# Strassen's algorithm in the up product of a squared-ReLU MLP

## The chip, the cores and the metric

The kernel runs on one core of a Trainium2 chip. The metric is the device time of one execution in microseconds (us); three executions of the kernel before took 1535.1, 1535.53 and 1536.06 us, and the median, 1535.53 us, is the time before. The profile is one more execution, taken by the hardware profiler; its own clock runs from the first to the last instruction (the span).

TensorE (PE) multiplies a stationary tile of 128x128 with a moving tile of 128 rows and up to 512 columns and adds into one of eight PSUM banks. VectorE (DVE), ScalarE (ACT) and GpSimd (POOL) do everything else; GpSimd works on SBUF only here. SyncE (SP) issues the loads.

## The reference

A trunk of two layers over 512 positions with 1024 channels, all in float32. Layer 0 mixes with a gated DeltaNet, layer 1 with a Conformer convolution; each layer then attends to a memory of 256 positions and ends in the MLP, which is what changes here:

```python
def sq_relu_mlp(h, w_up, w_down):      # w_up 1024 x 4096, w_down 4096 x 1024
    return jnp.square(jax.nn.relu(h @ w_up)) @ w_down

h = h + sq_relu_mlp(rms_norm(h, mlp_norm[layer]), mlp_w_up[layer], mlp_w_down[layer])
```

## The kernel before, in words

Activations lie transposed: a tile holds 128 channels (partitions) by 512 positions, so `h` is eight tiles. Every product is made of three fp32r matmuls (`mm3`, L227): each float32 operand is split into a high part, rounded to fp32r, and a low part, the rest. ACT writes the high part and DVE the low one: `split` (L264) for activations, `wsplit` (L199) for weights. So a product of one weight tile of 128x128 with one activation tile costs three matmuls of 512 columns, at the lines L229, L230 and L231.

**Weights.** All weight halves of the program stand in one list, `order`, in the order of their use. `wload` (L191) loads one of 512 KB (128x1024, eight stationary tiles, or 24 matmuls) into one of `NRAW`=3 buffers `raw`; `wsplit` turns it into `wh` and `wl`, of which there are `NW`=3 each. `wnext` (L217) hands out the next unit, and asks for loads `NRAW`+2 units and for splits `NW` units ahead. A buffer is given again when its last matmul is done, so a weight split in the trace is released by a matmul.

**MLP** (`mlp`, L960). The 4096 hidden channels are four groups of 1024. `MLP_ORDER` (L1426) runs up 0, up 1, down 0, up 2, down 1, up 3, down 2, down 3. An up step makes eight hidden tiles: 24 matmuls into one bank (`proj`, L237, over eight k-tiles), then `up_ev` (L966): DVE reads the bank, takes the positive part and multiplies it with the row `rb` of RMS factors; ACT squares; `split` makes `uh` and `ul`. A down step makes eight output tiles, 24 matmuls each, and DVE adds the bank to the residual. The RMS factor commutes with the product, so the up product starts on unnormalised activations: `Norm.parts` (L312) makes `xh`, `xl` (gain applied) as each residual tile appears at the end of the attention, and `stat` and `spread` compute `rb` while the first up tiles are multiplied.

**The last group** (`finish`, L1364). In layer 1 the last down step is done with positions on the partitions: eight outputs of 128 positions by 512 channels, each of four transposes (residual) and 24 matmuls, then the final norm and the store. Its weights are loaded and split by `load` (L1358) into the pool of general slots (`NSLOT`=69 tiles of 128x512).

The code is written in program order; a scheduler orders the instructions of each engine by that order and by its own estimate of when operands and buffers are ready, and sets all waits. The engines run their queues in order.

Of the kernel before, what the change touches and what calls it, by code (L numbers as in the profile page):

```python
# [14 lines left out]
P = 128  # L15
# [23 lines left out]
def tile_trunk(ctx, tc, xT, memT, prm_d, adt_d, bdw_d, tap_d, fin_d, w_ab, w_kq, w_v, w_z, w_dno, w_pw1, w_pw2,  # L39
# [159 lines left out]
    def wsplit():  # L199
        u = ws["split"]  # L200
        ws["split"] += 1
        while ws["load"] <= u:
            wload()
        raw = ws["raw"].pop(u)
        h = wp.tile([P, 1024], F32R, tag="wh", name=nm("wh"), bufs=NW)
        lo = wp.tile([P, 1024], F32R, tag="wl", name=nm("wl"), bufs=NW)
        ins = [act.copy(h, raw)]  # L207
# [7 lines left out]
        ws["hl"][u] = (h, lo)  # L215

    def wnext(key, hf):  # L217
# [9 lines left out]
    def mm3(ps, wk, xk, first, last):  # L227
        (wh, wl), (xh, xl) = wk, xk
        pe.matmul(ps, wh, xh, start=first, stop=False)  # L229
        pe.matmul(ps, wh, xl, start=False, stop=False)  # L230
        pe.matmul(ps, wl, xh, start=False, stop=last)  # L231
# [119 lines left out]


# [606 lines left out]

    def mlp(layer, norm, hres, nxt, mid=None, end=None, pre=None):  # L960
        xs = norm.xs
        hid = {}
        cur = list(hres)
        st = {"first": []}

        def up_ev(g, i, ps):  # L966
            t = slot(s="rl")
            stt(t, ps, 0.0, norm.rb, ALU.max, ALU.mult)
            u = slot(s="u2")
            act.activation(u, t, AF.Square)  # L970
            hid.setdefault(g, []).append(split(u, "u"))

        for kind, g in MLP_ORDER:
            if (kind, g) == ("dn", 3) and mid is not None:
                mid()
            if (kind, g) == ("dn", 3) and end is not None:
                return end(hid[3], cur)
            for i in range(8):
                w = wnext((kind, layer, g * 4 + i // 2), i % 2)
                ps = psum(kind)  # L980
                if kind == "up":
                    proj(w, xs, ps)
                    if g == 0 and i < 2:
                        st["first"].append(ps)
                        if i == 0:
                            norm.stat()
                        else:
                            norm.spread()
                            for j in range(2):
                                up_ev(0, j, st["first"][j])  # L990
                    else:
                        up_ev(g, i, ps)
                else:
                    proj(w, hid[g], ps)
                    if pre is not None and (g, i) in PRE:
                        pre()
                    hn = slot(s="h")
                    if g == 3:
                        tt(dve, by_phase(hn), phased(ps), phased(cur[i]), ALU.add)
                        nxt.add(i, hn)  # L1000
                    else:
                        tt(dve, hn, ps, cur[i], ALU.add)
                    cur[i] = hn
# [341 lines left out]
    n2 = Norm("mlp_norm0")  # L1345
# [5 lines left out]
    n5 = Norm("mlp_norm1")  # L1351
# [12 lines left out]
    def finish(hid, cur):  # L1364
        gt = fsp.tile([P, 1024], F32, tag="fs", name=nm("gt"))
        nc.sync.dma_start(out=gt, in_=fin_d.partition_broadcast(P))
        st = {}
        for c, g in LAST:
            if len(ws_) < 16:
                load()  # L1370
            cs, gs = slice(c * P, (c + 1) * P), slice(g * 512, g * 512 + 512)
            ps = psum("dn")
            for j in range(4):
                pe.matmul(ps[:, j * P:(j + 1) * P], cur[4 * g + j][:, cs], ident, is_transpose=True, start=j == 0, stop=False)
            for k in range(KT):
                (xh, xl), (h, lo) = hid[k], ws_[8 * g + k]
                pe.matmul(ps, xh[:, cs], h, start=False, stop=False)
                pe.matmul(ps, xl[:, cs], h, start=False, stop=False)
                pe.matmul(ps, xh[:, cs], lo, start=False, stop=k == KT - 1)
# [3 lines left out]
            if g == 0:  # L1383
# [4 lines left out]
                continue  # L1388
# [8 lines left out]

    mlp(1, n5, h, None, None, finish, load)


NSLOT = 69
NCV = 6
NRAW = 3
PRE = ((2, 4), (2, 6))
# [6 lines left out]
NW = 3  # L1411
# [14 lines left out]
MLP_ORDER = [("up", 0), ("up", 1), ("dn", 0), ("up", 2), ("dn", 1), ("up", 3), ("dn", 2), ("dn", 3)]  # L1426
# [12 lines left out]
def _pack_a(np, w, order=None):  # L1439
    t = _tiles_a(np, w)  # L1440
    if order is not None:
# [31 lines left out]
def _layout(np, i):  # L1473
# [34 lines left out]
    r["w_up"] = np.stack([_pack_a(np, i["mlp_w_up"][j]) for j in range(2)])  # L1508
# [20 lines left out]
```

## Time and profile before

| | |
|---|---|
| median of three executions | 1535.53 us |
| span of the profiled execution | 1533.4 us |
| PE busy | 1511.9 us, 99% |
| DVE, ACT, POOL busy | 900.1, 676.3, 228.7 us |
| mean granted PE clock | 0.996 |
| share of the 16 DMA engines | 29.6% |

The profile gives no time for the profiled execution beside its span; the median lies 2.1 us above that span, which is what comes before the first and after the last instruction.

A matmul's row shows its modelled duration; matmuls overlap, so what one of them costs is the distance between the starts of two that follow each other. The MLP of layer 0 runs from 492 us to 846 us, that of layer 1 from 1174 us to the end. In a row of the groups stand line, engine, operation, output and inputs, shape and count, then the sum in us and the mean in ns, then the idle time before and who ended it.

### The profile page before, as it was taken

The page shows a single profiled execution, that of the slowest core. Times are in us where ns is not written, and L with a number is a line of the kernel's source. Part 1 is how long each engine was busy: PE and PEld are TensorE (multiplying, and loading weights), DVE is VectorE, ACT ScalarE, POOL GpSimd, SP SyncE. Part 2 cuts the span into 40 slices and gives each one's busy share as a digit, 9 for nine tenths or more (in the row PEclk, how much of TensorE's full clock was granted, in tenths as well). Part 3 has the DMA queues.
Part 4 walks back from the last instruction along what each step waited for, and adds up shares of the span by engine and source line. Part 5 has one row for each costly group of instructions (what it writes and reads, how often), then busy time and mean ns, then how long its engine had stood idle before and what let it go on. Part 6 is the DMA issues. An engine that isn't in the chain of part 4 may idle for free.

```text
span 1533.4 us, 19367 instructions
## 1 busy us (share of the span) xinstructions
PE 1511.9 (99%) x7560; PEld 1274.0 (83%) x7560; DVE 900.1 (59%) x1372; ACT 676.3 (44%) x1089; POOL 228.7 (15%) x231
## 2 busy tenths in 40 slices
PE   9999999999999999999999999899999999999998
PEld 7888888988888888888888889878888888888886
DVE  6898898766545543443445599864554543434441
ACT  6847655655434442332324464363443441323332
POOL 1421220103112000000003685302112000000000
PEclk9999999999999999999999999999999999999999
DMA  5321123342213222222234524422212222232231
GB/s 179 100 82 62 60 76 111 124 152 82 74 37 110 96 97 97 96 96 97 96 109 150 180 85 149 155 95 96 74 51 97 97 96 97 96 98 97 99 106 55
DMA packets 49051, 153.56 MB, mean 100 GB/s; under 512 B 6208, under 2 KB 8000, under 8 KB 48960
## 3 DMA queue, kind: packets, MB, share of 16 engines
q1 hardware_dynamic: 48960, 152.33, 29.6%
q8 instruction: 59, 0.97, 0.2%
q14 instruction: 32, 0.26, 0.1%
HBM read 149.42 MB, written 2.10 MB: 99 GB/s over the span
## 4 chain that ended last, share of the span: by engine, by line
PE 78%; ACT 1%; DVE 1%; DMA 0%; POOL 0%; issue 0%; ACTq 0%; POOLq 0%; DVEq 0%
PE up L229 8%; PE up L231 8%; PE up L230 8%; PE dn L230 7%; PE dn L231 7%; PE dn L229 7%; PE pw L229 3%; PE pw L231 3%; PE pw L230 3%; PE q L229 2%; PE xo L230 2%; PE q L231 2%; PE q L230 2%; PE xo L229 2%; PE xo L231 2%; PE cv L1130 1%
## 5 line engine op out<-in xcount | busy, mean ns | idle before, releaser
L207 ACT CAST wh<-raw 128x1024 fp32r<-128x1024 f32 x248 | 260.0, 1051 | 627.3 <-PE dn L230 190.4
L70 DVE TENSOR_TENSOR wl<-raw,wh 128x1024 fp32r<-128x1024 f32 x224 | 275.9, 1233 | 96.3 <-ACT wh L207 94.7
L229 PE MATMUL up<-xh,wh 128*128 128x512 f32 x512 | 199.4, 389 | 0.0
L231 PE MATMUL up<-xh,wl 128*128 128x512 f32 x512 | 199.2, 389 | 0.0
L230 PE MATMUL up<-xl,wh 128*128 128x512 f32 x512 | 199.2, 389 | 0.0
L231 PE MATMUL dn<-uh,wl 128*128 128x512 f32 x448 | 174.3, 389 | 0.0
L229 PE MATMUL dn<-uh,wh 128*128 128x512 f32 x448 | 174.3, 389 | 0.0
L230 PE MATMUL dn<-ul,wh 128*128 128x512 f32 x448 | 174.3, 389 | 0.0
L70 DVE TENSOR_TENSOR h<-dn,h 128x512 f32<-128x512 f32 x56 | 41.8, 747 | 163.3 <-PE dn L231 163.3
L73 DVE SCALAR_TENSOR_TENSOR rl<-up,rb 128x512 f32<-128x512 f32 x64 | 44.2, 691 | 153.6 <-PE up L231 153.6
L70 POOL TENSOR_TENSOR sq<-sq,sq 128x512 f32<-128x512 f32 x30 | 48.6, 1621 | 470.1 <-ACT sq L321 470.1
L230 PEld LDWEIGHTS up<-xl,wh 128*128 128x128 f32 x512 | 96.1, 188 | 20.0
L231 PEld LDWEIGHTS up<-xh,wl 128*128 128x128 f32 x512 | 96.1, 188 | 20.0
L229 PEld LDWEIGHTS up<-xh,wh 128*128 128x128 f32 x512 | 96.1, 188 | 20.0
L229 PEld LDWEIGHTS dn<-uh,wh 128*128 128x128 f32 x448 | 84.1, 188 | 17.5
L230 PEld LDWEIGHTS dn<-ul,wh 128*128 128x128 f32 x448 | 84.1, 188 | 17.4
L231 PEld LDWEIGHTS dn<-uh,wl 128*128 128x128 f32 x448 | 84.1, 188 | 17.4
L73 DVE SCALAR_TENSOR_TENSOR ca<-x,prm,ca 128x512 f32<-128x512 f32 x120 | 87.9, 751 | 2.9 <-ACT ca L1093 1.3
L229 PE MATMUL h<-xh,wh 128*128 128x512 f32 x192 | 77.5, 404 | 1.2 <-ACT xh L314 1.2
L230 PE MATMUL h<-xl,wh 128*128 128x512 f32 x192 | 75.5, 393 | 0.6 <-DVE xl L73 0.6
L231 PE MATMUL h<-xh,wl 128*128 128x512 f32 x192 | 75.4, 393 | 0.0
L70 POOL TENSOR_TENSOR wl<-raw,wh 128x1024 fp32r<-128x1024 f32 x24 | 59.1, 2466 | 50.0 <-ACT wh L207 38.2
(348 smaller groups left out, 3068.0 us busy)
## 6 DMA issues: line engine op xcount, KB each, us to landing
raw<-w_up SPq DMA_DIRECT2D x64, 512.0 KB, 3.4
raw<-w_dn SPq DMA_DIRECT2D x64, 512.0 KB, 3.5
raw<-w_pw SPq DMA_DIRECT2D x24, 512.0 KB, 3.6
raw<-w_kq SPq DMA_DIRECT2D x16, 512.0 KB, 3.7
raw<-w_k SPq DMA_DIRECT2D x16, 512.0 KB, 3.8
raw<-w_vv SPq DMA_DIRECT2D x16, 512.0 KB, 3.8
raw<-w_q SPq DMA_DIRECT2D x16, 512.0 KB, 3.5
raw<-w_o SPq DMA_DIRECT2D x16, 512.0 KB, 3.5
```

Of the source, the lines that this page charges most:

```text
L70: return e.tensor_tensor(out=o, in0=a, in1=b, op=op)
L73: dve.scalar_tensor_tensor(out=o, in0=a, scalar=s, in1=b, op0=op0, op1=op1)
L207: ins = [act.copy(h, raw)]
L229: pe.matmul(ps, wh, xh, start=first, stop=False)
L230: pe.matmul(ps, wh, xl, start=False, stop=False)
L231: pe.matmul(ps, wl, xh, start=False, stop=last)
L1130: pe.matmul(o, x, TAPS[m][2 * j + u // 4][:, (u % 4) * P:(u % 4 + 1) * P], start=u == 0, stop=False)
```

## The change

The up product of a pair of hidden tiles (256 channels) is a product of 2x2 blocks: the weights A11, A12 (first hidden tile; even and odd k-tiles) and A21, A22 (second hidden tile), each four stationary tiles, and the activations B11, B12, B21, B22 (even or odd k-tile; positions 0-255 or 256-511), each 256 columns wide. The Winograd form of Strassen's algorithm makes it with seven block products instead of eight:

- `FormNorm.parts` replaces `Norm.parts` for the two MLPs. After each second residual tile it makes the activation forms B11, B21, B22, P1 = B11-B12, T3 = B22-B12, P2 and T4 (further sums), each as a high and a low part.
- `wforms` replaces `wsplit` for up weights. Per pair, POOL makes four sums of 128x512 (S2, S1, S3, S4), and `wpair` splits three blocks of 128x1024 and one of 128x512.
- `Up.run` does one block product: 4 k-tiles x 3 matmuls of 256 columns. Seven products go into three banks per pair: A takes the products 1, 6, 7 and 4 on top of each other, and is read after each of them; B takes 2; C takes 5 and then 3, and is read after 7 and after 3.
- The two hidden tiles of the pair are then made by `scalar_tensor_tensor` with `rb`, squared and split as before (the sign of the second is turned, and `min` taken for `max`).
- The order is written out: the seven products of four pairs a, b, c, d, interlaced, the first six k-tiles of three down tiles at the end of each group (`d006`), and the last down tile of the group before at its start (`d704p`). The groups run up 0, down 0, up 1, down 1 and so on. `finish` is cut into steps so that its first outputs fit into that order.
- Buffers: `NRAW` 3 to 4, `NW` 3 to 4 (splits are still asked for 3 units ahead, loads 6), `NSLOT` 69 to 70; the DMA scratch is set to 1024. The k-tiles of `w_up` are stored even ones first.

The core of the diff:

```diff
+    def wpair(src, names):
+        h = wp.tile([P, 1024], F32R, tag="wh", name=nm("wh"), bufs=NW)
+        lo = wp.tile([P, 1024], F32R, tag="wl", name=nm("wl"), bufs=NW)
+        act.copy(h, src)
+        tt(dve, lo, src, h.bitcast(F32), ALU.subtract)
+        return {n: (h[:, i * 512:i * 512 + 512], lo[:, i * 512:i * 512 + 512]) for i, n in enumerate(names)}
+
+    def wforms(raw, hf):
+        if hf == 0:
+            ws["first"] = raw
+            return wpair(raw, ("A11", "A12"))
+        top = ws.pop("first")
+        a11, a12, a21, a22 = top[:, 0:512], top[:, 512:1024], raw[:, 0:512], raw[:, 512:1024]
+        sa = fsp.tile([P, 1024], F32, tag="fs", name=nm("sa"))
+        sb = fsp.tile([P, 1024], F32, tag="fs", name=nm("sb"))
+        tt(pool, sa[:, 512:1024], a21, a22, ALU.add)
+        tt(pool, sa[:, 0:512], sa[:, 512:1024], a11, ALU.add)
+        r = wpair(sa, ("S2", "S1"))
+        tt(pool, sb[:, 0:512], a11, a21, ALU.add)
+        tt(pool, sb[:, 512:1024], sa[:, 0:512], a12, ALU.add)
+        r.update(wpair(sb, ("S3", "S4")))
...
+        r["A22"] = h, lo
+        return r
-        while ws["load"] < min(i + NRAW + 2, len(order)):
+        while ws["load"] < min(i + 6, len(order)):
-        while ws["split"] < min(i + (NW if i else 1), len(order)):
+        while ws["split"] < min(i + (3 if i else 1), len(order)):
...
+    class FormNorm(Norm):
+        def parts(self, t, h):
+            xg = slot(s="xg")
+            act.activation(xg, h, AF.Copy, scale=pc(self.g, t))
+            if t % 2 == 0:
+                self.even = xg
+                return
+            e, o = self.even, xg
+            b = slot(F32R, "xb")
+            act.copy(b[:, 0:256], e[:, 0:256])
+            tt(dve, b[:, 256:512], e[:, 0:256], b[:, 0:256].bitcast(F32), ALU.subtract)
+            g1, g2 = slot(s="g1"), slot(s="g2")
+            tt(dve, g1[:, 0:256], e[:, 0:256], e[:, 256:512], ALU.subtract)
+            tt(dve, g1[:, 256:512], o[:, 256:512], e[:, 256:512], ALU.subtract)
+            stt(g2[:, 0:256], g1[:, 0:256], -1.0, o[:, 256:512], ALU.mult, ALU.subtract)
+            stt(g2[:, 256:512], g2[:, 0:256], -1.0, o[:, 0:256], ALU.mult, ALU.subtract)
+            f = {"B11": (b[:, 0:256], b[:, 256:512])}
+            for src, n0, n1 in ((o, "B21", "B22"), (g1, "P1", "T3"), (g2, "P2", "T4")):
+                h_, l_ = split(src, "xf")
...
+    PAIR = {1: ("A", "A11", "B11", True), 2: ("B", "A12", "B21", True), 3: ("C", "S4", "B22", False),
+            4: ("A", "A22", "T4", False), 5: ("C", "S1", "P1", True), 6: ("A", "S2", "P2", False),
+            7: ("A", "S3", "T3", False)}
...
+        def run(self, n, p):
...
+            ps = s[bank][:, 0:256]
+            wh, wl = s["w"][wf]
+            for k in range(4):
+                c = slice(k * P, (k + 1) * P)
+                mm3(ps, (wh[:, c], wl[:, c]), self.norm.xs[k][xf], first and k == 0, k == 3, not first)
...
+            if n == 1:
+                act.copy(mu[:, lo], ps)
+            elif n == 2:
+                tt(dve, c1[:, lo], ps, mu[:, lo], ALU.add)
+            elif n == 6:
+                act.copy(mu[:, hi], ps)
+            elif n == 7:
+                act.copy(r[:, hi], ps)
+                tt(dve, r[:, hi], s["C"][:, 0:256], r[:, hi], ALU.add)
+            elif n == 4:
+                stt(r[:, lo], ps, 0.0, rb[:, lo], ALU.min, ALU.mult)
+                stt(r[:, hi], r[:, hi], 0.0, rb[:, hi], ALU.min, ALU.mult)
+                self.out(2 * p + 1, r)
+            elif n == 3:
+                tt(dve, c1[:, hi], ps, mu[:, hi], ALU.add)
+                stt(c1, c1, 0.0, rb, ALU.max, ALU.mult)
+                self.out(2 * p, c1)
...
-NSLOT = 69
+NSLOT = 70
-NRAW = 3
+NRAW = 4
-NW = 3
+NW = 4
-MLP_ORDER = [("up", 0), ("up", 1), ("dn", 0), ("up", 2), ("dn", 1), ("up", 3), ("dn", 2), ("dn", 3)]
+UP_TAIL = "7c 1d 2d 4c 6d 5d 3c 7d d006 4d d106 3d d206"
+UP_FIRST = "1a 5a 1b 5b 2a 6a stat 2b 6b spread 1c 7a 2c 7b 4a 6c 4b 5c 3a " + UP_TAIL.replace("7c ", "7c 3b ", 1)
+UP_SEQ = "d704p 1a 2a 6a d748p 5a 7a 1b 2b 4a 6b 5b 3a 7b 1c 2c 4b 6c 5c 3b " + UP_TAIL
+UP_LAST = UP_SEQ.replace("7c", "pre 7c").replace("5d", "pre 5d")
+MLP_ORDER = [(kind, g) for g in range(4) for kind in ("up", "dn")]
```

More of the change, by code (lines that the diff above doesn't have):

```diff
@@ L204, in wsplit @@
         raw = ws["raw"].pop(u)
+        if order[u][0][0] == "up":
+            ws["hl"][u] = wforms(raw, order[u][1])
+            return
         h = wp.tile([P, 1024], F32R, tag="wh", name=nm("wh"), bufs=NW)
@@ L1396, in finish, with step @@
             nc.sync.dma_start(out=yT[cs, 512:1024], in_=y)
+        def step(n, head):
+            if n is not None:
+                if n < 2:
+                    load()
+                mms(n, 0, 6)
+                return
+            gt = fsp.tile([P, 1024], F32, tag="fs", name=nm("gt"))
+            nc.sync.dma_start(out=gt, in_=fin_d.partition_broadcast(P))
+            st["gt"] = gt
+            for n in range(8):
+                mms(n, 6 if n < 3 else 0, KT)
+                out(n)
+        return step
     mlp(1, n5, h, None, None, finish, load)
-NSLOT = 69
+NSLOT = 70
 NCV = 6
-NRAW = 3
-PRE = ((2, 4), (2, 6))
+NRAW = 4
 DN_ORDER = (("k", 0), ("q", 0), ("z", 0), ("v", 0), ("k", 1), ("q", 1), ("z", 1), ("v", 1))
```

166 lines of the change are left out of this document (105 added, 61 removed).

## The prediction

> **What bounds the kernel now.** I read the page's head first, then the busy time by stretches, then the waits of PE, the groups by shape, and the timeline at a few places.
>
> ```profile
> span 1533.4 us, 19367 instructions
> PE 1511.9 (99%) x7560; PEld 1274.0 (83%) x7560; DVE 900.1 (59%) x1372; ACT 676.3 (44%) x1089; POOL 228.7 (15%) x231
> ```
> ```profile
> 541.00:628.00 87.00, 87.00 (x385) 72.06 (x384) 35.89 (x40) 26.09 (x32) 0.00 (x0) 1.00 0.29 97
> ```
> ```profile
> PE cvT L1114 <- ACT ca L1099: 4.7, 1, 4.7
> ```
>
> The second row is a stretch of up 1 and down 0 of layer 0 (columns PE, PEld, DVE, ACT, POOL, then clock, DMA share, GB/s). PE is busy throughout, at full clock; 384 matmuls in 87.00 us are 226.6 ns each. In the whole program PE is idle for 21.5 us (1533.4 - 1511.9), and its longest wait, 4.7 us, is in the Conformer. No wait of PE lies inside an MLP. So time here is the number of matmuls times their spacing, and DVE (35.89 of 87) and ACT (26.09) have room.
>
> **The price of a narrow matmul.** The change makes fewer multiplications but more matmuls: the question is what 256 columns cost. The trace has that shape, with weights stationary, in the memory's key projection.
>
> ```profile
> L229 PE MATMUL up<-xh,wh 128*128 128x512 f32 x512 | 199.4, 389 | 0.0
> L229 PE MATMUL K<-mh,wh 128*128 128x256 f32 x128 | 37.0, 289 | 0.0
> ```
> ```profile
> 950.05 0.28 PE L230 MATMUL K<-ml,wh 128*128 128x256 f32 x1
> ...
> 955.57 0.28 PE L231 MATMUL K<-mh,wl 128*128 128x256 f32 x1
> ```
>
> 47 matmuls start from the first to the last of these rows: 5.52 us / 46 = 120.0 ns. That is 6.7 ns over half of 226.6.
>
> Before: 3 x 512 = 1536 up matmuls x 226.6 ns = 348.1 us. After: 2 layers x 16 pairs x 7 products x 4 k-tiles x 3 = 2688 x 120.0 ns = 322.6 us. **PE: -25.5 us.** An eighth of the work would be 43.5 us; 18 go to the fixed part of each matmul (at 129.5 ns nothing would be left).
>
> [...]
>
> **What the other engines get.** The rows by which I price it:
>
> ```profile
> L207 ACT CAST wh<-raw 128x1024 fp32r<-128x1024 f32 x248 | 260.0, 1051 | 627.3 <-PE dn L230 190.4 <-PE up L230 184.2 <-issue 124.2
> L70 DVE TENSOR_TENSOR wl<-raw,wh 128x1024 fp32r<-128x1024 f32 x224 | 275.9, 1233 | 96.3 <-ACT wh L207 94.7
> L70 DVE TENSOR_TENSOR ul<-u,uh 128x512 fp32r<-128x512 f32 x64 | 44.3, 692 | 5.8 <-ACT uh L266 5.5
> L970 ACT ACTIVATE u<-rl 128x512 f32<-128x512 f32 x64 | 40.1, 626 | 9.6 <-DVE rl L73 9.6
> L266 ACT CAST uh<-u 128x512 fp32r<-128x512 f32 x64 | 39.8, 622 | 2.1
> L801 ACT COPY mrs<-mrs 128x256 f32<-128x256 f32 x1 | 0.4, 373 | 2.7 <-PE mrs L300 2.7
> L70 DVE TENSOR_TENSOR dg<-ident,vl 128x256 fp32r<-128x256 f32 x1 | 0.4, 422 | 0.0
> L70 POOL TENSOR_TENSOR sq<-sq,sq 128x512 f32<-128x512 f32 x30 | 48.6, 1621 | 470.1 <-ACT sq L321 470.1
> L70 DVE TENSOR_TENSOR h<-dn,h 128x512 f32<-128x512 f32 x56 | 41.8, 747 | 163.3 <-PE dn L231 163.3
> ```
>
> Per pair of hidden tiles, in us:
> - DVE: low parts of weights 3 x 1.23 + 0.69; five reads or products of 256 columns, 5 x 0.42; one of 512, 0.69; two `ul`, 1.38. Together 8.6 (before 2 x (1.23 + 0.69 + 0.69) = 5.2).
> - ACT: 3 x 1.05 + 0.62; three bank copies, 1.1; two squares and casts, 2.5. Together 7.4 (before 4.6).
> - POOL: four sums, 4 x 1.62 = 6.5 (before nothing).
>
> PE's own time for a pair is 7 x 12 x 0.12 = 10.1 us, so none of them is over it alone. But two share a road:
>
> ```profile
> 465.13 1.35 POOL L70 TENSOR_TENSOR sq<-sq,sq 128x512 f32<-128x512 f32 x1 [17.20 <-ACT sq L321]
> ...
> 831.83 2.39 POOL L70 TENSOR_TENSOR wl<-raw,wh 128x1024 fp32r<-128x1024 f32 x1 [2.37 <-ACT wh L207]
> 832.76 2.02 DVE L73 SCALAR_TENSOR_TENSOR xl<-h,prm,xh 128x512 fp32r<-128x512 f32 x1 [0.79 <-ACT xh L314]
> 834.17 1.75 POOL L70 TENSOR_TENSOR sq<-sq,sq 128x512 f32<-128x512 f32 x1
> ```
> ```profile
> L73 DVE SCALAR_TENSOR_TENSOR xl<-x,prm,xh 128x512 fp32r<-128x512 f32 x8 | 5.4, 748 | 0.0
> L73 DVE SCALAR_TENSOR_TENSOR ca<-x,prm,ca 128x512 f32<-128x512 f32 x120 | 87.9, 751 | 2.9 <-ACT ca L1093 1.3
> ```
>
> `xl`, two SBUF operands, takes 0.75 us alone and 2.02 beside a POOL sum: it ends half a us after POOL does. The POOL sum behind it takes 1.75 for 1.35. They run one after the other. `ca`, whose sum lies in PSUM, keeps 751 ns in the Conformer, where POOL is busy too. So POOL's time must be added to DVE's wherever DVE works on SBUF.
>
> Stretch by stretch: from `d704p` to `d206` a group takes PE 5.4 (down 7) + 40.3 (28 products) + 12.2 (54 matmuls) = 58.0 us. DVE has there 4 x 8.6, four down weights (4.9) and one residual (0.7): 40. POOL has 4 x 6.5 = 26 with contention, or 4 x 4 x 1.35 = 21.6 without. Were all of POOL's time lost to DVE, 62 to 66 us would stand against 58. But DVE is idle or reading PSUM for 18 + 7 of the 58 us, so some 0.57 of POOL's time (33/58), 15 us, should hit it: 55, no backlog. The sums of pair a can besides be made under the four down tiles before. A form is moreover split about 7 us ahead of its use: with four `wh` tiles, the block A of pair c finds the buffer of block A of b when `2b` ends, five products (7.2 us) before `1c`, and needs 1.05 + 1.23 us. **Steady stretch: 0, at most 8 us per group** (66 - 58).
>
> Bank A is read by ACT between its products. The tightest place is `1a 2a 6a`: one product, 1.44 us, for a copy of 0.37 that can sit behind a cast of 1.05. At most 0.2 us per group.
>
> What was covered and is no longer: before, up g+1 (43 us) lay between up g and down g. Now `u` of the last pair must be ready for the k-tiles 6 and 7 of `d0`. From the end of `3d`: bank read 0.42, product 0.69, square 0.63, cast 0.62, low part 0.69, with five hand-overs of about 0.15: 3.8 us. `d206` covers 4.1 us. **0.4 us per group, 3 in all** (0 to 2 each), since a cast of a down weight can come between.
>
> **Start of an MLP.** `FormNorm` makes the forms of the last residual tile in a longer chain, and `5a` needs P1 of the last k-tiles with the first 2.5 us of PE work (12 + 9 matmuls) as cover. The events of the last tile before the second MLP:
>
> ```profile
> 1174.16 0.69 DVE L70 TENSOR_TENSOR h<-xo,h 128x512 f32<-128x512 f32 x1 [2.65 <-PE xo L231]
> 1174.94 0.72 ACT L314 ACTIVATE xh<-h,prm 128x512 fp32r<-128x512 f32 x1
> 1175.07 1.23 DVE L70 TENSOR_TENSOR wl<-raw,wh 128x1024 fp32r<-128x1024 f32 x1 [0.21 <-ACT wh L207]
> ```
>
> After `wl` (1176.3) come T3 0.42, P2 and T4 0.84, and the low parts of B2x 0.69 and P1 0.69: 1178.9, where PE is there at 1176.4. The scheduler may draw `2a` or `1b` ahead. **+1.2 us per layer (0 to 2.5).** The statistics wait for nothing new, and `rb` is first wanted by product 4.
>
> **Moved loads.** Loads per pair stay two of 512 KB, on SP. The last group's own weights and the gain of the final norm come in other places of SP's list; the gain holds up DVE, not PE, as long as a bank is free. 0.
>
> **Buffers.** The fourth `raw` works elsewhere too. In the Conformer, ACT waits for a load that had to wait for a buffer, and behind it on ACT stands the copy that DVE wants before it can go on to the taps that PE's longest wait hangs on:
>
> ```profile
> 983.57 3.98 DMA raw<-w_vv
> 987.65 1.05 ACT wh L207
> 988.70 0.17 ACT cy L1118
> 988.90 0.30 DVE bn L1119
> ...
> 997.15 0.43 PE V L260
> ```
>
> This is the chain of waits. It continues to the transposes at 994.76, and after that pause matmuls of 512 columns stand 0.43 us apart for ten of them (0.23 else): 2 us more. One more buffer starts the load about a unit earlier. Whether the scheduler uses it so, no row shows: **-3 us**, about the middle between 0 and -6.7 (4.7 + 2).
>
> **Sum.** Span 1533.4 - 25.5 + 0.2 x 8 (bank A, its bound) + 3 + 2.4 - 3 = 1511.9; with the 2.1 us that the median lies above the span, **1514 us**. The likeliest case itself reaches from 1507 (no wait, the buffers give 3) to 1520 (half of the bounds of 16 and 5 for group ends and starts, nothing from the buffers).
>
> **Rivals.**
>
> *All hidden, and the Conformer's pause gone: 1504.* 1535.5 - 25.5 - 6.7 = 1503.3, plus 1 for what remains. For it: no wait of PE in either MLP now, and the written order leaves products between each read and the next use of a bank. Against: the scheduler doesn't see the shared road between POOL and DVE.
>
> *Ends of groups show: 1525.* If the chain from `3d` to `d0` finds DVE busy with the 1.23 us of a down weight and ACT with a cast of 1.05, it takes 3.8 + 2.3 = 6.1 against 4.1: 2 us in each of eight groups, 16 in place of 3, and 1514 - 3 + 16 - 2 (bank A's bound not met) = 1525. For it: both casts are due when `3c` and `3d` free their buffers. Against: they come before it in time, by the hand-over of 0.2 us.
>
> *DVE becomes the bound: 1550, slower.* Place: `d704p` to `d206`. If POOL's 26 us fall on DVE's SBUF work nearly always (0.9 of it), DVE has 40 + 23.4 = 63.4 us to do in 58; it ends the stretch 5.4 us late, the `u` tiles of the last pair come late by that less 0.3 of slack, 5 us in each of eight groups: 1535.5 - 25.5 + 40 = 1550. It decides from the point where 3.2 us per group (25.5 / 8) are lost, which is at 0.82 of POOL's time. For it: `xl` above, held for all of what POOL had left. Against: 0.57 by the idle time above. [...]
>
> *It doesn't do what it says: 1535.* If the 256-column stream can't hold 120 ns over a group because LDWEIGHTS or a bank that is being read holds it back (a semaphore at each of 28 products x 8 groups at 0.11 us makes 25), the gain is used up. For it: the fixed part of a matmul is already 13 ns of 120. Against: PE changes tiles 24 matmuls apart now with no such gap, and in the row of key projections too.
>
> **How the numbers follow.** Forecast 1514 (1507 to 1520): 0.50. All hidden, 1504 (1501 to 1507): 0.15. Group ends, 1525 (1520 to 1531): 0.20. Nothing gained, 1535: 0.05. DVE the bound, 1550: 0.10. A measurement of this kernel tells about 0.2%, 3 us, from no change. Faster by more: 0.50 + 0.15 + 0.20 = 0.85; within 0.2%: 0.05; slower: 0.10. The range of 8 in 10 leaves out the slower case and part of the nothing and of the fastest: 1502 to 1532.
>
> **What would show each step.** The spacing of `up` matmuls of 256 columns: 120 ns, and PE's stream about 25 us shorter. The stretch of a group: 83.8 us (40.3 + 43.5) for 87. PE's waits at `d0` for `u`: 0.4 us; 2 or more means the third case, 5 the slower one. `wl` in the MLP at 1.23 us mean; near 1.8 means that POOL falls on it. Wait of `up` for `xf` at an MLP's start: 0 to 2.5 us. The wait of `cvT` in the Conformer: shorter than 4.7. I am wrong if the spacing is over 125 ns, if PE waits over 3.2 us per group, or if another stage of the kernel, ordered anew by the scheduler with the new buffers, shifts by more than 7 us.

## The result and the profile after

The changed kernel takes 1561.44 us (median of four executions, 1553.73 to 1563.99), the kernel before 1535.32 us beside it (four, 1534.45 to 1536.06). The ratio is 1.016, with a 95% interval from 1.0135 to 1.0185: slower by 26 us, where 21.5 less were forecast (1514). The time lies outside the range and on the other side. The fastest of the four executions, 1553.73, has a mean granted clock of 0.989, the other three 0.981 to 0.983.

The head of the page after, and TensorE's longest waits (in us: total, times, longest):

```profile
span 1560.6 us, 22376 instructions
PE 1510.5 (97%) x8712; PEld 1324.2 (85%) x8712; DVE 1074.0 (69%) x1612; ACT 771.2 (49%) x1281; POOL 427.0 (27%) x359
```
```profile
PE upA L260 <- ACT r L1048: 11.7, 6, 2.0
PE upA L260 <- ACT xb L393: 11.4, 2, 5.8
PE upA L261 <- DVE xb L70: 2.8, 2, 1.4
PE cvT L1228 <- ACT ca L1213: 2.2, 1, 2.2
PE rb L331 <- DVE dg L70: 2.1, 2, 1.0
PE upC L260 <- ACT wh L223: 1.8, 2, 0.9
```

Before, no wait stood inside an MLP. Now there are two kinds: for `r`, the copy that empties bank A, in six places (groups 1 to 3 of both layers), and for `xb`, the form B11 of the activations, at the two starts. PE is idle for 50.1 us (1560.6 - 1510.5), 28.6 more than before.

The price of a matmul is not where the time went. From the timeline, two rows 26 matmuls apart:

```profile
610.15 0.28 PE L260 MATMUL upA<-xb,wh 128*128 128x256 f32 x1
...
613.27 0.28 PE L262 MATMUL upC<-xfh,wl 128*128 128x256 f32 x1
```

3.12 us / 26 = 120.0 ns, as forecast. But the distances from each of the 2688 up matmuls to the next start, added up over the timeline, are 376.9 us and not 322.6. I call the excess of 54.3 us the loss, and split it by place: **32.3 us in the first 32 us of the two MLPs (the starts), 22.0 us in the rest (the groups).** The median of the distances is 120 ns, so the loss lies in few of them.

The same stretch as in the prediction, then places where PE waits (columns PE, PEld, DVE, ACT, POOL, then granted clock, DMA share, GB/s):

```profile
541.00:628.00 87.00, 85.05 (x524) 77.09 (x523) 52.51 (x63) 35.46 (x51) 25.20 (x16) 0.98 0.31 97
492.00:496.70 4.70, 1.46 (x12) 1.26 (x11) 4.70 (x9) 3.33 (x5) 0.87 (x2) 1.00 0.26 97
496.70:513.70 17.00, 11.52 (x49) 10.64 (x50) 10.96 (x13) 6.62 (x13) 8.77 (x6) 0.50 0.10 33
612.00:616.00 4.00, 2.05 (x17) 1.85 (x17) 2.66 (x4) 2.08 (x4) 1.31 (x1) 1.00 0.38 131
616.00:619.60 3.60, 3.60 (x20) 3.60 (x19) 2.45 (x5) 0.66 (x2) 0.00 (x0) 0.53 0.18 51
```

DVE has 34 of 87 us free in a group (52.51 busy), and still PE waits. And with both pauses shown here goes a stretch at half clock: 17 us at the start of the MLP (0.50), 3.4 us behind the pause in the group (0.53). There the matmuls stand 0.21 us apart for 0.12.

**The wait in a group**, from the timeline (start, duration, engine; in brackets the idle time before and who ended it):

```profile
609.78 1.29 POOL L70 TENSOR_TENSOR sb<-raw,raw 128x512 f32<-128x512 f32 x1 [2.97 <-DVE wl L70]
609.96 2.20 DVE L70 TENSOR_TENSOR wl<-sb,wh 128x1024 fp32r<-128x1024 f32 x1
611.04 2.27 POOL L70 TENSOR_TENSOR sb<-sa,raw 128x512 f32<-128x512 f32 x1
612.08 1.77 DVE L73 SCALAR_TENSOR_TENSOR c<-c,rb 128x512 f32<-128x512 f32 x1
613.89 0.63 ACT L1062 ACTIVATE u<-c 128x512 f32<-128x512 f32 x1 [4.00 <-DVE c L73]
614.55 0.62 ACT L297 CAST uh<-u 128x512 fp32r<-128x512 f32 x1
615.07 0.36 ACT L1048 COPY r<-upA 128x256 f32<-128x256 f32 x1
615.49 0.39 PE L260 MATMUL upA<-xfh,ah 128*128 128x256 f32 x1 [1.95 <-ACT r L1048]
```

Read it from below. PE wants to write bank A (product 4 of pair b) and waits 1.95 us for its copy `r`. That copy wants only product 7, which ended at about 610.2: it lies ready for nearly 5 us. But on ACT it stands behind the Square of `c`, a tile of another product, and ACT, idle for 4.00 us, waits there for DVE. DVE brings `c` late because two of its instructions ran beside sums of POOL: 2.20 us, where the group of `wl` before the change had a mean of 1.23, and 1.77 us for a tile of 512 columns, which takes 0.69 to 0.75 in the prediction's rows. POOL's sum, too, took 2.27 us for some 1.35. So two holds of one us each on DVE become a pause of two us on PE, by way of an ACT that sits idle.

**The start of the MLP**, the last tiles of the attention's output:

```profile
487.62 1.55 DVE L70 TENSOR_TENSOR wl<-sa,wh 128x1024 fp32r<-128x1024 f32 x1 [1.71 <-ACT wh L223]
489.43 1.51 DVE L70 TENSOR_TENSOR xb<-xg,xb 128x256 fp32r<-128x256 f32 x1
490.86 1.51 DVE L70 TENSOR_TENSOR g<-xg,xg 128x256 f32<-128x256 f32 x1
...
497.11 0.68 DVE L70 TENSOR_TENSOR h<-xo,h 128x512 f32<-128x512 f32 x1
497.23 1.03 ACT L223 CAST wh<-raw 128x1024 fp32r<-128x1024 f32 x1
498.17 0.72 ACT L387 ACTIVATE xg<-h,prm 128x512 f32<-128x512 f32 x1
...
498.79 0.39 ACT L393 CAST xb<-xg 128x256 fp32r<-128x256 f32 x1
...
499.23 0.58 PE L260 MATMUL upA<-xb,wh 128*128 128x256 f32 x1 [5.77 <-ACT xb L393]
```

The last product of `xo` ended at 491.4 (the first up matmul starts there); its residual add stands at 497.11. DVE runs without a break from 489 on, and is 5.7 us behind: on its list are the forms of earlier tiles, the low parts of the weights and instructions that POOL's sums stretch (`xb` and `g` of 256 columns 1.51 us, for 0.42 in the version without sums, below). So everything that hangs on the last residual tile is late, and PE pauses 5.77 us.

### The profile page after: what moved, and what is told of

The parts are those of the page before. It is cut to its first block, busy times and chain, and to the rows that moved or that the text cites. A ratio compares the mean times of both kernels' runs of the same rounds, so it can differ in the third digit from the quotient of the medians.

```text
span 1560.6 us, 22376 instructions
## 1 busy us (share of the span) xinstructions
PE 1510.5 (97%) x8712; PEld 1324.2 (85%) x8712; DVE 1074.0 (69%) x1612; ACT 771.2 (49%) x1281; POOL 427.0 (27%) x359
## 5 line engine op out<-in xcount | busy, mean ns | idle before, releaser
L210 ACT CAST wh<-raw 128x1024 fp32r<-128x1024 f32 x184 | 192.2, 1048 | 237.5 <-issue 67.0
L70 DVE TENSOR_TENSOR wl<-raw,wh 128x1024 fp32r<-128x1024 f32 x192 | 250.1, 1305 | 76.2 <-ACT wh L210 63.4
L70 POOL TENSOR_TENSOR sa<-raw 128x512 f32<-128x512 f32 x32 | 44.4, 1386 | 347.1 <-DMA raw<-w_up 322.0
L261 PEld LDWEIGHTS dn<-ul,wh 128*128 128x128 f32 x448 | 84.2, 188 | 15.9
L70 DVE TENSOR_TENSOR ul<-u,uh 128x512 fp32r<-128x512 f32 x64 | 44.2, 691 | 61.2 <-ACT uh L297 60.6
L70 DVE TENSOR_TENSOR al<-raw,ah 128x512 fp32r<-128x512 f32 x32 | 34.3, 1071 | 63.7 <-ACT ah L242 63.4
L260 PE MATMUL upA<-xfh,wh 128*128 128x256 f32 x256 | 76.4, 299 | 0.0
L260 PE MATMUL upC<-xfh,wh 128*128 128x256 f32 x256 | 74.3, 290 | 1.8 <-ACT wh L223 1.8
L261 PE MATMUL upA<-xfl,wh 128*128 128x256 f32 x256 | 75.8, 296 | 0.0
L262 PE MATMUL upA<-xfh,wl 128*128 128x256 f32 x256 | 75.7, 296 | 0.0
L261 PE MATMUL upC<-xfl,wh 128*128 128x256 f32 x256 | 74.5, 291 | 1.2 <-DVE xfl L70 1.2
L262 PE MATMUL upC<-xfh,wl 128*128 128x256 f32 x256 | 73.8, 288 | 0.0
```

The source lines that it names most:

```text
L70: return e.tensor_tensor(out=o, in0=a, in1=b, op=op)
L260: pe.matmul(ps, wh, xh, start=first, stop=False, skip_group_check=more)
L261: pe.matmul(ps, wh, xl, start=False, stop=False, skip_group_check=more)
L262: pe.matmul(ps, wl, xh, start=False, stop=last, skip_group_check=more)
```

## Experiments

Two theories stood after reading the traces. **Theory:** the matmuls are as cheap as forecast, and what is lost comes from POOL's sums, which make DVE late at a few places; queues that work in order carry it to PE, and the half clock behind the pauses adds to it (17.4 of the 54.3 us by the distances, as the section on the prediction shows). **Rival:** the loss belongs to the structure (short banks, long forms, DVE's own list), whoever makes the sums. Below, "loss" is always the excess over 120 ns per up matmul, at starts and in groups, in the one profiled execution of each version. The half clock in it can be longer or shorter from one execution to the next (mean granted clock 0.981 to 0.989 in the four of the changed kernel), so a difference of a few us at the starts says little.

| kernel | us | ratio to before, 95% | loss at starts | in groups |
|---|---|---|---|---|
| changed kernel | 1561.44 | 1.016 [1.0135, 1.0185] | 32.3 | 22.0 |
| no sums | 1518.51 | 0.9887 [0.9872, 0.9902] | 7.9 | 3.0 |
| sums on DVE | 1526.24 | 0.9937 [0.9922, 0.9952] | 15.9 | 2.7 |
| few forms | 1538.28 | 1.0014 [1.0004, 1.0024] | 8.8 | 23.7 |
| copy first | 1547.86 | 1.0083 [1.0066, 1.01] | 26.0 | 10.4 |
| sums and squares on DVE | 1527.46 | 0.9938 [0.9923, 0.9953] | 16.9 | 2.8 |
| and forms made earlier | 1531.91 | 0.9974 [0.9965, 0.9984] | 19.2 | 2.7 |
| sums on DVE, those of pair b later | 1522.18 | 0.9908 [0.9891, 0.9924] | 10.1 | 2.7 |
| and 1a 2a first | 1523.78 | 0.992 [0.9905, 0.9935] | 11.9 | 2.7 |
| pair b and the spread later | 1518.78 | 0.989 [0.9874, 0.9907] | 7.4 | 2.9 |
| the same and copy first, sums on POOL | 1544.25 | 1.0053 [1.0037, 1.0068] | 26.2 | 10.4 |

### No sums

```diff
-        tt(pool, sa[:, 512:1024], a21, a22, ALU.add)
-        tt(pool, sa[:, 0:512], sa[:, 512:1024], a11, ALU.add)
-        r = wpair(sa, ("S2", "S1"))
+        r = wpair(top, ("S2", "S1"))
...
-        r.update(wpair(sb, ("S3", "S4")))
+        r.update(wpair(raw, ("S3", "S4")))
```

> The four GpSimd sums per pair are left out: S2, S1, S3 and S4 are split from the raw weight blocks, so the output is not the reference's; all else stays. Theory 'shared road' (the sums hold VectorE up, its backlog delays the bank copies and the first forms, PE pauses and its clock is halved for a while): the low parts of weights fall back to 1.23 us mean, the six waits of 1.95 us at bank A and most of the 19 us of waits at the two MLP starts go, and so does most of the half-clock time; 1508 to 1520 us. Rival 'length' (the chains through VectorE and ScalarE are too long in themselves, whoever makes the sums): 1550 to 1562 us.

1518.51 us. The products are split from the raw blocks here, so the output is not the reference's. No wait of a us or more for `r` or for the first half of `xb` (line 393 of the changed kernel, 387 here) is left (0.5 and 0.6 us at most), and the mean granted clock is 0.998, for 0.981 in the changed kernel. The second half of `xb` takes 417 ns again, where its mean in the changed kernel is 1230 ns; by the groups of this kernel:

```profile
L70 DVE TENSOR_TENSOR xb<-xg,xb 128x256 fp32r<-128x256 f32 x8 | 3.3, 417 | 1.0 <-ACT xb L387 1.0
```

43 us hang on the sums; without them the change would bring 17 us. What stays is 10.9 us of loss and the forecast's stream.

### Sums on VectorE

```diff
-        tt(pool, sa[:, 512:1024], a21, a22, ALU.add)
+        tt(dve, sa[:, 512:1024], a21, a22, ALU.add)
...
-        tt(pool, sb[:, 512:1024], sa[:, 0:512], a12, ALU.add)
+        tt(dve, sb[:, 512:1024], sa[:, 0:512], a12, ALU.add)
```

> The same four sums on VectorE in place of GpSimd: 4 x 0.69 = 2.8 us more on VectorE per pair, nothing left on GpSimd but the norm's sums. Theory 'shared road': 2.8 us of its own cost VectorE less than 5.4 to 6.5 us of GpSimd that it waits for; the waits at bank A go or shrink, 1518 to 1540 us. Rival 'load' (VectorE's own work is what is too much): worse than the change, 1565 us or more.

1526.24 us, faster than before. The same sums on the engine that is busiest beside TensorE cost 8 us over none at all; on POOL they cost 43. So of the 43 us, 35 hang on which engine makes the sums. The groups are clean (2.7 us of loss), though DVE now does everything itself. Of the groups of this kernel (columns of the groups as in the prediction), a sum on DVE and on POOL in the changed kernel:

```profile
L70 DVE TENSOR_TENSOR sb<-sa,raw 128x512 f32<-128x512 f32 x32 | 21.9, 683 | 0.0
```
```profile
L70 POOL TENSOR_TENSOR sb<-sa,raw 128x512 f32<-128x512 f32 x32 | 53.1, 1661 | 0.6
```

683 ns of DVE's time against 1661 ns during which DVE can be held. The slower sum could also cost by its own lateness, as weight forms that come too late; that is not what happens, for TensorE's waits for `wh` in the up products are 1.8 us in the changed kernel and 2.0 us here. The starts still lose 15.9 us, by the first of the waits of this kernel:

```profile
PE upA L260 <- ACT xb L393: 7.8, 2, 4.3
```

### The buffers alone

The kernel before, with four `raw` and four `wh`, `NSLOT` 70, loads six and splits three units ahead, and the DMA scratch of the change; nothing else.

```diff
...
-NSLOT = 69
+NSLOT = 70
-NRAW = 3
+NRAW = 4
...
-NW = 3
+NW = 4
...
```

> The kernel before with only the buffers of the change: 4 raw and 4 wh/wl tiles, 70 slots, loads 6 and splits 3 units ahead. By the prediction's term: 3 us less than before (0 to 6.7), the wait of cvT below 4.7 us; 1529 to 1535.5 us. Rival: another order of the scheduler eats it, within 0.2% of before.

1530.78 us (ratio 0.9967, 0.9956 to 0.9979), 4.9 us less than the 1535.67 beside it. The pause in the Conformer:

```profile
PE cvT L1114 <- ACT ca L1099: 2.2, 1, 2.2
```

4.7 became 2.2, and the mean granted clock 0.998 for 0.996. So up to 5 us of what any of these versions gains over before has nothing to do with Strassen. In the changed kernel the stretches outside the two MLPs are 3.9 us shorter than before.

### Few forms

`FormNorm` makes only B11 and the split of the odd tile; P1, T3, P2 and T4 are left out, and the products use the split of the odd tile in their place; the output is not the reference's.

```diff
-            g1, g2 = slot(s="g1"), slot(s="g2")
-            tt(dve, g1[:, 0:256], e[:, 0:256], e[:, 256:512], ALU.subtract)
...
-            for src, n0, n1 in ((o, "B21", "B22"), (g1, "P1", "T3"), (g2, "P2", "T4")):
-                h_, l_ = split(src, "xf")
+            h_, l_ = split(o, "xf")
+            for n0, n1 in (("B21", "B22"), ("P1", "T3"), ("P2", "T4")):
```

> FormNorm without the forms P1, T3, P2 and T4 (the blocks B21 and B22 stand in for them, so the output is not the reference's): per pair of residual tiles 3 us less on VectorE and 1.2 us less on ScalarE, GpSimd's sums stay. Theory 'backlog at the start' (VectorE is late with the last residual tiles because it also makes the forms and the weights' low parts): the waits of the two MLP starts fall from 19 to under 8 us and their half-clock time with them, 1530 to 1548 us; the six waits of 1.95 us stay. Rival 'the start is GpSimd's alone': 1555 to 1562 us.

1538.28 us: 23 us of the changed kernel's time are in the starts, and go when DVE has about a quarter of the forms' work (0.41 + 0.69 us per pair of tiles, for 5 x 0.41 + 3 x 0.69), with POOL still summing. The groups are untouched:

```profile
PE upA L260 <- ACT r L1043: 11.7, 6, 2.0
```

The two places are thus separate, and at the starts both DVE's own list and POOL's hold on it count: taking away the sums or most of the forms leaves a quarter of the loss there (7.9 and 8.8 us).

### ScalarE's copy first

`self.late` gathers the Squares and splits of `c` of three pairs, and they are issued behind the next copy of bank A.

```diff
-                act.copy(r[:, hi], ps)
+                ins = act.copy(r[:, hi], ps)
+                with tc.issue_after(getattr(ins, "ins", ins)):
+                    for args in self.late:
+                        self.out(*args)
+                self.late = []
...
-                self.out(2 * p, c1)
+                if p < 3:
+                    self.late.append((2 * p, c1))
+                else:
+                    self.out(2 * p, c1)
```

> The changed kernel with one edit in the order of ScalarE's instructions: the Square and the split of `c` of the first three pairs of a group are issued behind the copy `r<-upA` of the next product 7, not ahead of it. GpSimd still makes the sums. Theory (ScalarE works in order, and the copy that frees bank A stands behind a Square which waits for a late VectorE): the six waits of TensorE for `r` at line 1048, 11.7 us together, go, and with them the five 3.41 us half-clock stretches in the groups, about 8 us; waits and clock at the two MLP starts stay; the time is 1540 to 1546 us. Rival (VectorE is behind as a whole and the copy's place is chance): the waits come back under another name (`mu`, `c` or `u`) at the same places, and the time stays at 1555 to 1563 us.

1547.86 us, 2 us over the range of the theory. The waits of this kernel:

```profile
PE upA L260 <- ACT xb L393: 11.1, 2, 5.6
PE upA L260 <- ACT mu L1043: 5.3, 6, 0.9
```

and its timeline at the place of the wait above:

```profile
608.80 0.37 ACT L1049 COPY r<-upA 128x256 f32<-128x256 f32 x1 [0.45 <-PE upA L262]
612.36 0.63 ACT L1070 ACTIVATE u<-c 128x512 f32<-128x512 f32 x1 [3.19 <-DVE c L73]
613.55 0.36 ACT L1043 COPY mu<-upA 128x256 f32<-128x256 f32 x1
613.97 0.39 PE L260 MATMUL upA<-xfh,wh 128*128 128x256 f32 x1 [0.90 <-ACT mu L1043]
```

The copy `r` runs at once. ACT waits for DVE as long as before (3.19 for 4.00 us), and the next bank copy, `mu`, pays for it, with 0.9 us for 1.95. So both were right in part: ACT's order is what carried the delay to PE, and DVE's delay is still there and finds the next copy; another 2.4 us of waits arise at the down products, for `uh`. The loss in the groups falls from 22.0 to 10.4 us. At the starts it falls from 32.3 to 26.0 us though the waits are nearly the same (11.1 us for `xb` in place of 11.4) and the edit does not touch that place; the mean granted clock of this execution is 0.991, that of the changed kernel's 0.981.

### The norms' squares on VectorE, and forms made earlier

Two attempts on the start, on top of the sums on DVE. First the sums of squares of the two MLP norms go from POOL to DVE; then, beside that, B11 and P1 are made and split when the even tile of a pair is there.

```diff
-    n2 = FormNorm("mlp_norm0")
+    n2 = FormNorm("mlp_norm0", dve)
-    n5 = FormNorm("mlp_norm1")
+    n5 = FormNorm("mlp_norm1", dve)
```

> The kernel with the weight sums on VectorE, and beside that the sums of squares of the two MLP norms moved from GpSimd to VectorE. Theory (what makes VectorE late at an MLP start is GpSimd sharing its road, not VectorE's own list): `wl` and `xb` at the starts take 1.23 and 0.41 us again, the two waits of TensorE for `xb` of line 393 (4.3 us mean) fall under 2 us each, the two half-clock stretches go, and the time is 1517 to 1523 us. Rival (VectorE's own list at the start is too long, and the squares make it longer): the waits stay at 3 to 5 us each, and the time is 1525 to 1531 us.

```diff
-                self.even = xg
+                e = xg
+                b, g1, p1 = slot(F32R, "xb"), slot(s="g1"), slot(F32R, "xp")
+                act.copy(b[:, 0:256], e[:, 0:256])
...
+                tt(dve, g1[:, 0:256], e[:, 0:256], e[:, 256:512], ALU.subtract)
+                act.copy(p1[:, 0:256], g1[:, 0:256])
```

> The version before this in the list (sums and the norms' squares on VectorE), and the forms B11 and P1 are made and split as soon as the even one of two residual tiles is there, not with the odd one. Theory (the start waits for the first form of the last pair of tiles, and the forms stand in one burst at the end): the waits for `xb` at the MLP starts go to under 1 us each; 1514 to 1520 us, the nearest to the 1510 us that are left when the forecast's stream saving stands alone. Rival (the burst is bounded by VectorE's sum of work, not by its order): no change against the version before it within 1.5 us.

1527.46 us, no different from 1526.24. The waits for `xb` fall to 0.8 us each, as the theory had it, but the half clock doesn't go (mean granted clock 0.992, for 0.996 with the sums on DVE), and the time is the rival's, since another wait has come behind them:

```profile
PE upC L261 <- DVE xfl L70: 4.1, 2, 2.0
```

The forms made earlier give 1531.91 us (0.9974, 0.9965 to 0.9984), slower than that by 4.5 us, which neither theory had:

```profile
PE upA L260 <- ACT mu L1049: 8.0, 2, 4.0
```

More pieces and splits on both engines before the end of the attention, and now a bank's copy stands behind them. Both misses fit one reading: once POOL's sums are gone, the start is bounded by how much DVE and ACT have to do before the last residual tile's forms, and neither edit took anything away from that. The later versions, which move sums out of the time before those forms, gain.

### POOL's sums in the kernel before

The kernel before, with two sums of 128x512 per half of an up weight into tiles that nobody reads, as many as the change has.

```diff
+        if order[u][0][0] == "up":
+            t = fsp.tile([P, 1024], F32, tag="fs", name=nm("sx"))
+            for i_ in range(2):
+                tt(pool, t[:, i_ * 512:i_ * 512 + 512], raw[:, 0:512], raw[:, 512:1024], ALU.add)
```

> The kernel before with two sums of 128x512 on GpSimd added to each of the weight blocks of the up products, four to a pair of tiles as in the change, written to tiles that nobody reads; its products and its order are as before. Theory (what costs is a late VectorE in front of a short-lived bank, and the kernel before has no such bank: 512 columns to an eviction and two banks): `wl` gets longer than 1.23 us, but TensorE waits little, and the time is 1535 to 1543 us. Rival (GpSimd on VectorE's road costs TensorE's time in any structure): 1550 to 1565 us, with waits of 15 us or more at the MLP starts and in the groups.

1536.52 us, ratio 1.0002 (0.9992 to 1.0011): no change. Two of its groups and the longest of TensorE's waits:

```profile
L70 DVE TENSOR_TENSOR wl<-raw,wh 128x1024 fp32r<-128x1024 f32 x224 | 304.7, 1362 | 89.4 <-ACT wh L211 88.0
L70 POOL TENSOR_TENSOR sx<-raw 128x512 f32<-128x512 f32 x128 | 222.9, 1762 | 294.7 <-DMA raw<-w_up 294.7
```
```profile
PE cvT L1118 <- ACT ca L1103: 5.1, 1, 5.1
```

POOL works 220 us more, DVE's low parts of weights grow from 1233 to 1362 ns and its `ul` from 692 to 1130, and no wait arises in an MLP. DVE, with the same instructions, is busy for 969.8 us in place of 900.1, so 0.32 of POOL's added time fell on it. In the changed kernel it is 1074.0 us against 1015.0 without the sums, 59 us for 203 of POOL: 0.29. The hold on DVE is thus about as large in both kernels; it costs TensorE nothing here and 43 us there. What differs is the structure: in the changed kernel a late DVE meets a bank that is wanted again after two or three products, and a longer list at the start. That these two are the places is shown by the versions with the copy first and with few forms; a run that changed the life of the banks alone was not made. So the loss needs both, POOL's hold on DVE and a structure that has no room for it.

### The sums of the second pair behind the last forms

On the version with the sums on DVE: the sums of the second pair are issued behind the last form of the last residual tile.

```diff
+        if hf == 1 and hold:
+            ins = hold[-1]
+            hold.clear()
+            with tc.issue_after(getattr(ins, "ins", ins)):
+                return wforms(raw, hf)
...
+                if t == 7:
+                    hold.append(last_split[0])
```

> The kernel with the weight sums on VectorE (1526 us), and one edit in VectorE's order: the sums of the second pair of each MLP's first group are issued behind the forms of the last residual tile, not ahead of its residual add. Theory (at the MLP start TensorE waits for `xb` because VectorE, in order, is 4 us behind when the last `xo` product is there): the waits of TensorE for `xb` (7.8 us in two) go under 1.5 us each; but product 5 of pair b now comes before its sums, and waits 2 to 4 us for `wh`; so 1523 to 1529 us. Rival (the forms themselves set the start): the waits for `xb` stay, 1526 to 1531 us.

1522.18 us, a little under the theory's range. The waits for `xb` are gone, the mean granted clock is 0.997 (0.996 with the sums on DVE in their old place), and the feared wait for `wh` doesn't come: the start loses 10.1 us for 15.9. The residual add now stands where it can be, in the timeline of the version below:

```profile
491.70 0.69 DVE L70 TENSOR_TENSOR h<-xo,h 128x512 f32<-128x512 f32 x1 [0.42 <-PE xo L269]
```

It was at 497.11 in the changed kernel and at 495.26 with the sums on DVE in their old place. Then the first products in another order, so that those without weight sums come first:

```diff
-UP_FIRST = "1a 5a 1b 5b 2a 6a stat 2b 6b spread 1c 7a 2c 7b ...
+UP_FIRST = "1a 2a 1b 2b 5a 6a stat 5b 6b spread 1c 7a 2c 7b ...
```

> The version before this in the list, and the products of the first group's first two pairs in the order 1a 2a 1b 2b 5a 6a 5b 6b, so that those which need no sum of weights come first. Theory (both lists, of forms and of sums, are then out of TensorE's way at the start): no wait of more than 1.5 us at the MLP starts, no half-clock stretch there; 1514 to 1520 us, at or under the 1518.5 us of the kernel that makes no sums. Rival (VectorE's work at the start has no room in any order): a wait of 3 us or more turns up at another operand (`xfl`, `wh` or `r`), 1523 to 1530 us.

1523.78 us (0.992, 0.9905 to 0.9935), nothing gained. The time is the rival's; the wait is 2.5 us each, under its 3, and at an operand it did not name:

```profile
PE rb L338 <- DVE dg L70: 5.0, 2, 2.5
```

### The spread later, and the same with POOL's sums

Back to the order of the products of the change, with the spread of `rb` two products later:

```diff
-UP_FIRST = "1a 5a 1b 5b 2a 6a stat 2b 6b spread 1c 7a 2c 7b ...
+UP_FIRST = "1a 5a 1b 5b 2a 6a stat 2b 6b 1c 7a spread 2c 7b ...
```

> The version with the sums on VectorE and behind the last forms (1522 us), and one move: the spread of the norm's reciprocal (`rb`) comes two products later, behind 7a. Theory (what is left at the MLP start are single short waits, each at an operand that VectorE or ScalarE brings late, `rb` <- `dg` being the longest): the two waits of 1.3 us for `dg` go, 1518 to 1521.5 us. Rival (VectorE's list is full, and a later product waits in its place): 1521.5 to 1524 us.

**1518.78 us, ratio 0.989 (0.9874 to 0.9907): faster than the kernel before and the changed one,** and level with the version that makes no sums. Its group stretch and the largest wait left in the MLPs:

```profile
541.00:628.00 87.00, 86.95 (x541) 78.27 (x540) 56.92 (x82) 37.66 (x54) 0.00 (x0) 1.00 0.30 97
```
```profile
PE upC L268 <- DVE xfl L70: 1.7, 2, 0.9
```

DVE is busier than in the changed kernel (56.92 for 52.51 us), POOL not at all, and PE does 541 matmuls in the 87 us for 524.

Last, this version with the sums put back on POOL and ACT's copies first, that is, the change with these order edits:

```diff
-        tt(dve, sa[:, 512:1024], a21, a22, ALU.add)
+        tt(pool, sa[:, 512:1024], a21, a22, ALU.add)
...
```

> The version before this in the list with the weight sums back on GpSimd, as the change has them, and with ScalarE's copies of bank A ahead of the Squares as in the earlier run (1548 us): both order edits, sums on GpSimd. Theory (GpSimd on VectorE's road makes the start late whatever the order): waits of TensorE for `xb` of 3 us or more at both MLP starts stay, with half-clock stretches; 1536 to 1548 us. Rival (the orders were all of it): the waits at the starts go under 1.5 us each, 1519 to 1528 us.

1544.25 us, with the start nearly as bad as in the changed kernel (26.2 us of loss for 32.3); its longest wait, and the stretch of the start:

```profile
PE upA L267 <- ACT xb L400: 10.9, 2, 5.4
```
```profile
497.00:514.00 17.00, 12.60 (x54) 11.72 (x55) 11.57 (x15) 6.89 (x13) 7.38 (x5) 0.50 0.24 77
```

Time and waits are the theory's: these two edits do not mend the start while POOL sums. But "whatever the order" is not shown, because the order of the sums themselves did not change. The edit puts instructions behind one of DVE's and so moves DVE's part alone; two sums of the second pair on POOL, from the timeline of this kernel:

```profile
475.99 2.27 POOL L70 TENSOR_TENSOR sa<-raw 128x512 f32<-128x512 f32 x1
...
489.68 1.40 POOL L70 TENSOR_TENSOR sb<-raw,raw 128x512 f32<-128x512 f32 x1 [1.16 <-DVE wl L70]
```

They stand where they stood in the changed kernel (476.17 and 489.25), ahead of the last residual add (497.54), while on DVE they had moved behind the forms (497.31). POOL's sums held back in the same way were not tried.

## Why the prediction was wrong, step by step

- **PE's stream, -25.5 us: right.** 120.0 ns, and 2688 x 120.0 = 322.6 of the 376.9 us. The price read off the key projection carried over to another place and to banks that are written in turns.
- **Buffers, -3 us: right in kind,** -4.9 measured alone; outside the MLPs the changed kernel is 3.9 us shorter.
- **From `3d` to `d0`, 3 us: not there.** Among the changed kernel's waits there is none of `dn` for `uh`.
- **Bank A, "at most 0.2 us per group": failed.** I took one product (1.44 us) as cover and a cast of 1.05 us as the worst that can stand ahead of the copy. What stands ahead of it is an instruction that itself waits for DVE. It cost six waits of 1.95 us. I had named the copy's duration and its queue, and had not asked what the instructions in the queue wait for. With the half clock behind them, 22.0 us stand against a bound of 1.6.
- **Steady stretch, "0, at most 8 us per group", "no backlog": failed, and not by its total.** The 0.57 of POOL's time on DVE was even too much: 59 of 203 us fell on it, 0.29, and DVE has 34 us free in the 87. Nor did the sign that I had named come, a mean of `wl` near 1.8 us: the groups of `wl` made from `raw`, `sb` and `sa` have means of 1305, 1549 and 1241 ns. A mean hides a few long holds. The step from "no backlog over 58 us" to "no wait" was wrong. Two held instructions in a row are enough where the hand-over from `c` to `u` to `r` has 3 us to spare. An average over a stretch says nothing of that.
- **Start, +1.2 us per layer (0 to 2.5): failed by far.** 32.3 us of loss in two starts. I worked from the row at which the residual add stood in the trace of before, 1174.16, and added the forms behind it. But the list before it is a different one. Ten us ahead of the first MLP, before and after:

```profile
480.00:490.00 10.00, 10.00 (x46) 8.29 (x45) 5.16 (x6) 4.39 (x6) 2.91 (x2) 1.00 0.23 79
```
```profile
480.00:490.00 10.00, 10.00 (x45) 8.26 (x44) 8.29 (x14) 5.93 (x10) 4.87 (x3) 1.00 0.19 60
```

  DVE had half of these 10 us free; now 8.29 are taken, and all of the 4.70 from 492 on (above). With the forms of earlier tiles, the weights' splits and POOL's sums of the first two pairs, which are made just there, the add itself comes 5.7 us late. The end of a list was counted, not the list.
- **The clock: left out of the sum.** In the Conformer I had priced the half clock behind a pause ("2 us more"), and put it into none of the waits that I expected. By the distances, some 17 of the 54.3 us are matmuls that wait for nothing and run at half clock: 187 distances of 185 to 240 ns, 17.4 us over 120 ns each.
- **The sum,** by the two traces: -25.5 + 32.3 + 22.0 + 2.4 (the distances of the down matmuls sum to 354.2 for 351.8 us, many of them a few ns longer and none at half clock) - 3.9 (outside the MLPs) = +27.3. The spans differ by 27.2, the medians by 26.1.
- **The rivals.** The slower one named the cause, POOL's sums on DVE's road, but put it at the end of a group, as a sum of DVE's time, with 0.82 of POOL's time as the point from which it decides. It decided with far less. What its `xl` showed, 2.02 for 0.75 us beside a POOL sum, was to be weighed more: `wl` took 2.20 for 1.23 us here. With the sums moved from POOL to DVE 35 us went. The hold alone does not explain the loss, as the sums in the kernel before show (ratio 1.0002).

## What to carry to other kernels

Work given to GpSimd to spare VectorE is not free just because GpSimd is idle: price each of its instructions as a possible hold on VectorE (here `xb` took 1.51 us for 0.42 beside a sum of 1.41), and look for the one place where a held VectorE is followed, over in-order queues, by a bank that TensorE wants back soon. Test slack at the tightest hand-over and at the starts and ends of stages, counting the whole list of the engine there and not the last chain; and put the half clock behind a pause into the price of the pause (here 17.4 of 54.3 us). Here the same sums on VectorE itself, late in its order, made the change worth 17 us, of which up to 5 are buffers.

## What was not expected of the hardware

- A pause of about 2 us can be enough for half clock. Of the six waits of 1.95 us in the changed kernel five were followed by a stretch of 3.41 us at half clock, and one, of the same length, was not:

```profile
1399.16 0.38 PE L260 MATMUL upA<-xfh,ah 128*128 128x256 f32 x1 [1.96 <-ACT r L1048]
```
```profile
1399.00:1402.00 3.00, 2.84 (x23) 2.84 (x24) 2.97 (x6) 1.33 (x3) 0.00 (x0) 1.00 0.00 0
```

  What decides between the five and the sixth is open, as is how long the half clock lasts behind a start: in the changed kernel each of the two has 17.07 us of it, with waits of 5.77 and 5.61 us, while with the sums on DVE the clock is 0.90 from 497 to 514 us, with a wait of 3.55 us, so about 3.4 us of it (an estimate, 2 x 0.10 x 17.00).
- A sum on GpSimd and an instruction of VectorE with two SBUF operands hold each other: 1.77 us for 0.69 to 0.75 on VectorE, 2.27 for 1.35 on GpSimd, in the changed kernel. Over a whole kernel 0.29 (the change) and 0.32 (the kernel before with sums) of GpSimd's added time fell on VectorE, and in the kernel before that cost TensorE nothing (1536.52 us, ratio 1.0002).
